# Data work of GpSimd moved to the vector and scalar engines in a two-block transformer kernel

## The chip, the cores and the metric

The kernel runs on one core of a Trainium2 chip. The metric is the device time of one execution in microseconds (us), the median of several runs. TensorE (PE) multiplies matrices, VectorE (DVE) and ScalarE (ACT) work on rows of 128 partitions, GpSimd (POOL) can do the same arithmetic, and SyncE (SP) issues most DMAs. Each engine works off its own queue of instructions in order, and engines wait for each other by semaphores.

## The reference, cut to what matters

The input is 256 tokens of 1024 numbers in single precision. A first block has two layers, each of a feed-forward part, an attention mixer, a second feed-forward part and a gate; a second block has a mixer of attention and a spatial gate, a cross attention to a memory of 256 rows, and then an expert layer that takes a third of the time:

```python
def peer_ffn(h, w_q, subkeys, w_down, w_up):          # 16384 experts, 8 heads, 16 experts per head and token
    q = (xc @ w_q).reshape(128, 8, 2, 128)
    s = jnp.einsum("thpd,hpnd->thpn", q, subkeys)
    s1, i1 = lax.top_k(s[:, :, 0], 16)
    s2, i2 = lax.top_k(s[:, :, 1], 16)
    cand_s = s1[..., :, None] + s2[..., None, :]
    cand_i = i1[..., :, None] * 128 + i2[..., None, :]
    top_s, top_pos = lax.top_k(cand_s, 16)            # over the 256 candidates of a head
    e = jnp.take_along_axis(cand_i, top_pos, axis=-1)
    g = softmax(top_s)
    a = gelu(einsum("td,thkd->thk", xc, w_down[e]))
    return einsum("thk,thkd->td", g * a, w_up[e])
```

Before every part stands a norm, `x * rsqrt(mean(x*x) + 1e-6) * g`.

## The kernel before, in words

All matrices are multiplied in three passes: a weight is split into a rounded half `wH` (ACT, a copy) and the rest `wL` (DVE, weight minus `wH`), the activations likewise into `xH` and `xL`, and PE adds `xH wH + xH wL + xL wH`. Weights come in pieces of 128 x 1024 through four buffers `raw`; `split` (L1360) makes the halves, `prefetch` two pieces ahead. The tokens are two tiles of 128, whose units of work are interleaved by `run_units` (L1381).

`rsqrt` (L475) computes a reciprocal root on one number per partition in nine small GpSimd instructions: an integer guess and three Newton steps. It follows `sumsq` (L532), a squaring on ACT that also sums. `rsqrt2` (L489) does two at once. There are 33 roots on POOL, 29 single ones and two pairs, and one on DVE; `fin1` (L1071) chains two of them for each tile, since the final norm of the first block and the first norm of the second stand one behind the other.

The expert layer does not gather. It multiplies all 16384 experts: 128 down items ("D", 24 matmuls of 256 columns each, then a gelu) and 128 up items ("U", 12 matmuls of 512 columns), with a coefficient matrix that is zero where a token did not choose an expert. For the first 96 items (`DAHEAD`, L31) there are only D items; from the 97th on, U and D alternate. During these 96 items the choice of the experts and the coefficients are computed beside the matmuls, as background units:

- `peer_sel` (L1550), for each tile of tokens: `pick` (the best 16 of 128 of the second half of the heads), `cand` (50 of the 256 candidates of a head are enough; their scores `c` and indices `e`), `top` (the best 16 of 50), `exps`, `soft`, and per head `dec` (L1596: compare the position with a counter, 16 x 50 = 800 wide, on DVE, then multiply by `e` on POOL) and `red` (a sum on DVE); `fin` and `finT` make, transposed, the indices `idx` in 16 bits and the weight split into a power of two `pow` and two half-precision parts of its mantissa.
- `peer_coef` (L1654), for each group of four tokens, 64 groups: `hot` (L1663) makes one-hot rows on DVE: a comparison of 1024 wide in 16 bits into `X` (tag `pTs`), two products of 512 into `Y` (tag `qT`), a product with `pow` of 512; `prod` (L1683) has eight small matmuls on PE, an eviction on ACT into `KT`, and after every fourth group a DMA of the coefficients to DRAM from ACT's queue.
- `prep` (L1710), for each U item: coefficient times activation (POOL, 256 wide, tag `qT`), then the split on ACT and DVE (tag `pTs`). The coefficients come back from DRAM by `load_coef` (L1705), a DMA on SP, for eight items at a time.

As long as background units are left, `split` gives 384 (`SHARE`, L38) of a piece's 1024 columns of `wL` to POOL (L1369 to L1372).

When the units are issued follows `background` (L1746): a model of three engines' free times, with costs per unit, `BG` and `SLACK`, advanced by 2.6 us for each item. Every instruction is recorded in that order; then `Plan.order` (L297) puts all of them in a final order for each engine. It simulates the engines with the costs of `times` (L202) and takes, whenever an engine is free, the instruction with the lowest number that is ready. SP's DMAs keep their order. Only the order is kept from this; on the chip, semaphores decide.

At the end, `finish`, `finish_r` and `finish_out` (L1831 to L1859) add the result, take the last norm and store it; the root of tile 0 is on POOL, that of tile 1 on DVE.

All instructions are emitted by one helper (L150), so the profile tells them apart by tile names: `wL<-raw,wH` is a split.

Of the kernel before, what the change touches and what calls it, by code (L numbers as in the profile page):

```python
# [6 lines left out]
F = mybir.dt.float32  # L7
# [24 lines left out]
BG = 1.35, 1.2, 1.4  # L32
SLACK = 3.0
# [4 lines left out]
SHARE = 384  # L38
# [163 lines left out]
def times(i):  # L202

    views = i.outs + i.reads
    n = max(columns(v) for v in views)
    small = min(size(v.dtype) for v in views) == 2
    ps = any(v.buf.space == "ps" for v in i.reads)
    if i.op == "dma_start":
        return 330, 0
    if i.eng == "tensor":  # L210
        n = columns(i.outs[0])
        if i.op == "transpose":
            return 109, 272
        if i.a[1].dtype == F:
            return (223, 388) if n > 64 else (200, 380)
        if n < 256:
            return 112, 290
        return 0.4427 * n + 5.8, 0.43 * n + 172
    if i.eng == "vector":
        if i.op in ("max", "max_index", "match_replace"):  # L220
            b = n + 60
        elif i.op in ("tensor_scalar", "tensor_copy") and not ps:
            b = 0.54 * n + 120 if n > 4 else 80
        elif small:
            b = 0.53 * n + 65
        elif n <= 32:
            b = n + 80
        else:
            b = 1.04 * n + (80 if i.op == "tensor_tensor_reduce" or not ps else 110)
        return b, b + (85 if n > 4 else 90)  # L230
    if i.eng == "scalar":
        b = 0.833 * n + (190 if "accum_out" in i.k else 100)
        return b, b + (10 if "accum_out" in i.k else 105)
    b = 2.3 * n + 250
    return b, b
# [155 lines left out]
class Body:  # L391
# [83 lines left out]
    def rsqrt(self, ss, n, out, g=None):  # L475

        g = g or self.nc.gpsimd
        w = self.sb([128, 4], F, "rsq", 3)
        g.tensor_scalar(w[:, 0:1], ss, 1.0 / n, EPS, op0=OP.mult, op1=OP.add)
        g.tensor_scalar(w[:, 2:3].bitcast(I32), w[:, 0:1].bitcast(I32), -0.5, float(0x5F3759DF),  # L480
                        op0=OP.mult, op1=OP.add)
        g.tensor_scalar(w[:, 1:2], w[:, 0:1], -0.5, None, op0=OP.mult)
        y = w[:, 2:3]
        for i in range(3):
            g.tensor_scalar(w[:, 3:4], y, y, w[:, 1:2], op0=OP.mult, op1=OP.mult)
            z = out if i == 2 else w[:, 2:3]
            g.tensor_scalar(z, w[:, 3:4], 1.5, y, op0=OP.add, op1=OP.mult)

    def rsqrt2(self, ss, ns, out):  # L489

        g = self.nc.gpsimd
        w = self.sb([128, 8], F, "rsq2", 2)
        v, xh, u = w[:, 0:2], w[:, 2:4], w[:, 4:6]
        for i in range(2):
            g.tensor_scalar(v[:, i:i + 1], ss[:, i:i + 1], 1.0 / ns[i], EPS, op0=OP.mult, op1=OP.add)
        g.tensor_scalar(out.bitcast(I32), v.bitcast(I32), -0.5, float(0x5F3759DF), op0=OP.mult, op1=OP.add)
        g.tensor_scalar(xh, v, -0.5, None, op0=OP.mult)
        for i in range(3):
            g.tensor_tensor(u, out, out, op=OP.mult)
            g.tensor_tensor(u, u, xh, op=OP.mult)  # L500
            g.tensor_scalar(u, u, 1.5, None, op0=OP.add)
            g.tensor_tensor(out, out, u, op=OP.mult)
# [29 lines left out]
    def sumsq(self, src, n, ss=None):  # L532
        ss = self.sb([128, 1], F, "ss", 4) if ss is None else ss
        self.nc.scalar.activation(self.slot("junk", 1, 512).bitcast(mybir.dt.bfloat16)[:, :n], src, AF.Square,
                                  accum_out=ss)
        return ss

    def half_rs(self, t):

        self.hr[t] = self.sb([128, 1], F, "hrs", 2)  # L540
        self.nc.gpsimd.tensor_scalar(self.hr[t], self.rs[t], 0.5, None, op0=OP.mult)

    def norm(self, t, name, src=None, rname="rs", pre=PRE, post=POST, tags="pa", fn=None, half=False):
# [12 lines left out]
        def stats(_):  # L556
            ss = self.sumsq(self.h[t] if src is None else src(t), 1024)
            self.rs[t] = self.sb([128, 1], F, f"{rname}{t}", 2)
            self.rsqrt(ss, 1024, self.rs[t])
# [1482 lines left out]
```

## Time and profile before

| | us |
|---|---|
| median of 3 runs | 2174.52 (2174.11 to 2177.05) |
| the profiled execution's own time | 2176.68 |
| its span, first to last instruction | 2174.9 |
| PE busy | 2105.7 (97%) |
| DVE busy | 1360.5 (63%) |
| ACT busy | 1158.9 (53%) |
| POOL busy | 433.1 (20%) |

The busy time of PE counts matmuls that overlap: the next begins before the last has drained. So a PE that is busy all the time can still be slower than its best pace, and the pace is read from how many matmuls a stretch holds. The mean of one DVE or ACT instruction likewise holds up to about 0.1 us in which its successor already runs.

### The profile page before, as it was taken

The numbers are of one execution on the slowest core, as the hardware profiler recorded it, in microseconds if no ns is written. First come the engines' busy times: TensorE is split into PE (matmuls) and PEld (weight loads), VectorE is DVE, ScalarE is ACT, GpSimd is POOL, SyncE is SP. The second block draws the span as 40 slices with busy tenths as digits, with TensorE's granted clock in tenths as the row PEclk, the third lists the DMA queues.
The fourth block names the chain that finished last, engine by engine and source line by source line (L and its number), as shares of the span: only waits on it lengthen the run. The fifth ranks groups of instructions, "written<-read, shape, count | busy, mean of one in ns | idle before, by whom it ended". The sixth has DMA issues, their size and how long they took to land.

```text
span 2174.9 us, 31356 instructions
## 1 busy us (share of the span) xinstructions
PE 2105.7 (97%) x11616; PEld 1775.6 (82%) x11616; DVE 1360.5 (63%) x2445; ACT 1158.9 (53%) x1787; POOL 433.1 (20%) x589
## 2 busy tenths in 40 slices
PE   8999999999999999999999999987999999999997
PEld 6888778887888887888778888887999999888886
DVE  5555655557555565555755667999979645455554
ACT  5445754446444665444655565544667544444454
POOL 1001110004000101000330112367446311122222
PEclk9999999999999999999999999999999999999999
DMA  6655336565665443666544654344767867677783
GB/s 224 210 184 167 115 116 188 183 189 174 193 184 179 148 140 101 194 184 188 192 146 141 189 164 146 107 146 156 245 208 243 265 208 226 206 230 244 230 254 125
DMA packets 138379, 398.59 MB, mean 183 GB/s; under 512 B 12912, under 2 KB 47344, under 8 KB 135920
## 3 DMA queue, kind: packets, MB, share of 16 engines
q1 hardware_dynamic: 135920, 379.80, 56.2%
q10 hardware_dynamic: 2304, 16.78, 2.2%
q8 instruction: 91, 1.49, 0.3%
q14 instruction: 64, 0.52, 0.1%
HBM read 378.71 MB, written 17.83 MB: 182 GB/s over the span
## 4 chain that ended last, share of the span: by engine, by line
PE 84%; DVE 10%; ACT 2%; issue 2%; POOL 1%; DMA 0%; SPq 0%; ACTq 0%; POOLq 0%; DVEq 0%
PE m L150 44%; PE a L150 35%; PE p L150 5%; DVE wL L150 2%; DVE pTs L150 2%; DVE qT L150 2%; DVE V L150 1%; POOL rsq L150 1%; DVE C L150 1%; DVE E L150 1%; ACT wH L150 1%; ACT xH L150 0%; ACT s L150 0%; DVE xL L150 0%; DVE junk L150 0%
## 5 line engine op out<-in xcount | busy, mean ns | idle before, releaser
L150 DVE TENSOR_TENSOR wL<-raw,wH 128x1024 fp32r<-128x1024 f32 (+2 forms) x678 | 807.1, 1193 | 634.7 <-ACT wH L150 632.4
L150 ACT ACTIVATE wH<-raw 128x1024 fp32r<-128x1024 f32 (+1 forms) x678 | 715.4, 1058 | 745.9 <-PE a L150 332.2
L150 PE MATMUL m<-wH,xH 128*128 128x512 f32 (+1 forms) x1088 | 447.4, 411 | 14.4 <-DVE s L150 5.9
L150 PE MATMUL m<-wH,xL 128*128 128x512 f32 (+1 forms) x1088 | 432.7, 398 | 0.9 <-DVE xL L150 0.9
L150 PE MATMUL m<-wL,xH 128*128 128x512 f32 (+1 forms) x1088 | 432.5, 398 | 0.9 <-DVE wL L150 0.9
L150 PE MATMUL a<-wH,pTs 128*128 128x512 f32 x1024 | 326.1, 394 | 0.0
L150 PE MATMUL m<-xH,wL 128*128 128x256 f32 x1024 | 290.4, 284 | 24.3 <-DVE wL L150 19.8
L150 PE MATMUL m<-xH,wH 128*128 128x256 f32 x1024 | 293.5, 287 | 0.0
L150 PE MATMUL m<-xL,wH 128*128 128x256 f32 x1024 | 287.8, 281 | 1.0 <-DVE xL L150 1.0
L150 PE MATMUL a<-wH,s 128*128 128x512 f32 (+1 forms) x760 | 265.8, 394 | 0.0
L150 PEld LDWEIGHTS m<-wH,xH 128*128 128x128 f32 x1088 | 206.8, 190 | 62.9 <-DVE s L150 7.4
L150 PEld LDWEIGHTS m<-wH,xL 128*128 128x128 f32 x1088 | 206.6, 190 | 49.4 <-DVE xL L150 1.5
L150 PEld LDWEIGHTS m<-wL,xH 128*128 128x128 f32 x1088 | 207.4, 191 | 42.4 <-DVE wL L150 2.0
L150 PEld LDWEIGHTS a<-wH,pTs 128*128 128x128 f32 x1024 | 192.3, 188 | 44.2
L150 POOL TENSOR_SCALAR rsq<-ss 128x1 f32<-128x1 f32 x33 | 10.9, 331 | 1089.0 <-ACT junk L150 1088.3
L150 PEld LDWEIGHTS m<-xH,wL 128*128 128x128 f32 x1024 | 193.8, 189 | 29.3 <-DVE wL L150 24.0
L150 PE MATMUL a<-wL,pTs 128*128 128x512 f32 x512 | 202.0, 394 | 0.0
L150 PEld LDWEIGHTS m<-xL,wH 128*128 128x128 f32 x1024 | 194.5, 190 | 2.9 <-DVE xL L150 1.4
L150 PEld LDWEIGHTS m<-xH,wH 128*128 128x128 f32 x1024 | 193.6, 189 | 1.4
L150 POOL TENSOR_TENSOR wL<-raw,wH 128x384 fp32r<-128x384 f32 x90 | 147.9, 1651 | 148.2 <-ACT wH L150 125.0
L150 PEld LDWEIGHTS a<-wH,s 128*128 128x128 f32 x760 | 142.5, 188 | 32.7 <-ACT E L150 0.6
L150 PE MATMUL a<-wL,s 128*128 128x512 f32 (+1 forms) x380 | 149.1, 392 | 0.0
(272 smaller groups left out, 2433.0 us busy)
## 6 DMA issues: line engine op xcount, KB each, us to landing
raw<-in_ws_dram SPq DMA_DIRECT2D x416, 512.0 KB, 3.7
raw<-in_wdn_dram SPq DMA_DIRECT2D x128, 512.0 KB, 3.7
raw<-in_wup_dram SPq DMA_DIRECT2D x128, 512.0 KB, 4.3
coef<-KT ACTq DMA_DIRECT2D x16, 1024.0 KB, 5.0
KT<-coef SPq DMA_DIRECT2D x16, 1024.0 KB, 7.9
raw<-in_ws_dram SPq DMA_DIRECT2D x4, 416.0 KB, 3.2
h<-in_x_dram SPq DMA_DIRECT2D x4, 256.0 KB, 5.1
stage<-in_alibi_dram SPq DMA_DIRECT2D x1, 1024.0 KB, 8.1
```

What stands on the lines that cost most here:

```text
L150: return getattr(getattr(nc, self.eng), self.op)(*[v.get() if isinstance(v, View) else v for v in self.a], **real)
```

## The change

Every POOL instruction that works on data in SBUF goes to another engine, except those that prepare constants (`memset`, `gfin`, the triangle of the spatial gate):

- The reciprocal root: eight DVE instructions instead of nine on POOL; the mean is already formed by ACT's squaring (`scale`), so the first step falls away, and pairs are two single roots. In `fin1` the second root is taken of a product with `other`, so that it does not wait for the first.
- The split: DVE subtracts all 1024 columns; `SHARE` is gone.
- `cand`: the nine sums of `e` go to DVE. `dec`: the comparison is made in 16 bits, its product with `e` goes to DVE.
- `hot`: the product with `pow` becomes four ACT instructions of 128 columns, each with `pow` as its scale; `pow` is kept in single precision.
- `prep`: the product goes to DVE. `xn` (a scaled copy in `peer_q`) goes to ACT. The products with the last gain in `finish`, the two small steps of the sink in `attn`, and tile 0's last root go to DVE.
- The background: instead of the model of three engines, one list (selection of tile 0; then groups of four tokens, the first 32 of them with tile 1's selection between them) of which after each item so much is issued that the DVE costs of the units are spread evenly over 90 items (`DAHEAD - SPARE`). `load_coef(0)` comes at item 93; before, three items behind the last unit.
- `times` has new costs for the order: for instance no extra price for an ACT eviction into `KT`, 97 ns for each per-partition scalar operand on ACT.

The core of the diff:

```diff
+    if i.eng == "scalar":
+        b = (0.833 * n + 50 if ps else 0.86 * n + 87) + 97 * each
...
-    def rsqrt(self, ss, n, out, g=None):
-        g = g or self.nc.gpsimd
+    def rsqrt(self, ms, out, other=None):
+        v = self.nc.vector
         w = self.sb([128, 4], F, "rsq", 3)
...
+        m, y, z = w[:, 0:1], w[:, 1:2], w[:, 2:3]
+        if other is None:
+            v.tensor_scalar(m, ms, EPS, -0.5, op0=OP.add, op1=OP.mult)
+        else:
+            v.tensor_scalar(z, other, EPS, EPS, op0=OP.add, op1=OP.mult)
+            v.tensor_scalar(m, ms, z, -0.5, op0=OP.add, op1=OP.mult)
+        v.tensor_scalar(y.bitcast(I32), m.bitcast(I32), -0.5, float(0x5F3759DF - 2 ** 30 - 2 ** 22),
                         op0=OP.mult, op1=OP.add)
         for i in range(3):
...
+            v.tensor_scalar(z, y, y, m, op0=OP.mult, op1=OP.mult)
+            v.tensor_scalar(out if i == 2 else y, z, 1.5, y, op0=OP.add, op1=OP.mult)
...
-        d = w - self.share
-        nc.vector.tensor_tensor(l[:, :d], src[:, :d], h[:, :d].bitcast(F), op=OP.subtract)
-        if self.share:
-            nc.gpsimd.tensor_tensor(l[:, d:], src[:, d:], h[:, d:].bitcast(F), op=OP.subtract)
+        nc.vector.tensor_tensor(l, src, h.bitcast(F), op=OP.subtract)
...
+                nc.vector.tensor_tensor(hit.rearrange("p k (c d) -> p k c d", d=2),
+                                        cut(self.iob[:, :NC], 2).unsqueeze(1).to_broadcast(wide),
+                                        V["tb"][:, 16 * h:16 * h + 16].unsqueeze(2).to_broadcast(wide),
                                         op=OP.is_equal)
-                nc.gpsimd.tensor_tensor(eq, eq, V["e"][:, h, :].unsqueeze(1).to_broadcast([128, 16, NC]), op=OP.mult)
+                nc.vector.tensor_tensor(eq, hit, V["e"][:, h, :].unsqueeze(1).to_broadcast([128, 16, NC]), op=OP.mult)
...
-                nc.vector.tensor_tensor(x[:, :4], x[:, :4], V["pow"][:, c].unsqueeze(2).to_broadcast(half), op=OP.mult)
+                for i in range(4):
+                    nc.scalar.activation(X[:, i, :], X[:, i, :], AF.Copy, scale=V["pow"][:, c.start + i:c.start + i + 1])
...
-        nc.gpsimd.tensor_tensor(cut(ca, 16), cut(self.act.pop(j), 16), self.cb[j // 8][:, :, j % 8, :],
+        nc.vector.tensor_tensor(cut(ca, 16), cut(self.act.pop(j), 16), self.cb[j // 8][:, :, j % 8, :],
                                 op=OP.mult)
...
+        back = s0 + [f0]
         s1.append(f1)
+        for q, u in enumerate(Hs):
+            back += [u] + s1[len(s1) * q // 32:len(s1) * (q + 1) // 32] + ([Ps[q - 1]] if q else [])
+        back.append(Ps[-1])
+        whole, spent = sum(u.cost[0] for u in back), 0.0
+        def background(part):
+            nonlocal spent
+            while back and spent <= part * whole:
+                spent += back[0].cost[0]
+                back.pop(0).fn(None)
...
+            if m < DAHEAD - 1:
+                background((m + 1) / (DAHEAD - SPARE))
+            if m == DAHEAD - SPARE + 3:
                 self.load_coef(0)
```

## Rows read from the trace of the kernel before

**Rows 1.** The page: busy time of each engine.
```profile
PE 2105.7 (97%) x11616; PEld 1775.6 (82%) x11616; DVE 1360.5 (63%) x2445; ACT 1158.9 (53%) x1787; POOL 433.1 (20%) x589
```

**Rows 2.** Windows: stretch, length, busy time (instructions) of each engine, clock, DMA.
```profile
core 0: us, PE busy (x) PEld busy (x) DVE busy (x) ACT busy (x) POOL busy (x), PEclk, DMA share, GB/s
1374.18:1716.48 342.30, 315.89 (x2833) 307.33 (x2832) 316.64 (x670) 198.80 (x233) 195.00 (x130) 0.99 0.62 203
1568.58:1581.95 13.37, 13.37 (x132) 13.20 (x130) 13.16 (x21) 9.13 (x11) 6.78 (x4) 1.00 0.70 237
1699.59:1713.65 14.06, 14.06 (x122) 14.06 (x121) 6.61 (x6) 7.37 (x10) 3.05 (x3) 1.00 0.98 329
1716.48:2164.00 447.52, 447.35 (x2306) 378.85 (x2304) 239.30 (x288) 215.87 (x305) 96.19 (x127) 1.00 0.70 218
...
1374.18:1444.60 70.42, 61.52 (x493) 58.77 (x492) 69.45 (x235) 33.11 (x45) 45.70 (x39) 1.00 0.47 150
```

**Rows 3.** Waits of PE in 1374.18 to 1716.48: total us, times, longest.
```profile
PE m L150 <- DVE wL L150: 19.8, 19, 3.0
```

**Rows 4.** DVE by form, 1374.18 to 1444.6: busy us, mean ns | idle before.
```profile
L150 DVE TENSOR_TENSOR wL<-raw,wH 128x640 fp32r<-128x640 f32 x19 | 22.6, 1187 | 0.0
L150 DVE TENSOR_TENSOR E<-c_iota,V 128x800 f32<-128x800 f32 x8 | 11.1, 1392 | 0.0
```

**Rows 5.** DVE by form, 1380 to 1720.
```profile
L150 DVE TENSOR_TENSOR qT<-pTs,rope 128x512 f16<-128x512 bf16 x128 | 73.4, 614 | 0.3
L150 DVE TENSOR_TENSOR pTs<-c_mask,rope 128x1024 bf16<-128x1024 bf16 x64 | 51.8, 810 | 1.8 <-PE p L150 1.4
```

**Rows 6.** Chain of waits, 1460 to 1530: start us, us, what.
```profile
1466.42 0.59 DVE pTs L150
1467.01 0.74 DVE wL L150
1467.75 0.67 DVE qT L150 x2
...
1496.49 0.98 DVE E L150
```

**Rows 7.** Chain of waits, 525 to 537: a whole split; timeline at 1566.
```profile
529.63 1.14 DVE wL L150
...
1566.17 0.82 DVE L150 TENSOR_TENSOR wL<-raw,wH 128x640 fp32r<-128x640 f32 x1
```

**Rows 8.** The page: POOL's first step of a root; POOL by form: its splits.
```profile
L150 POOL TENSOR_SCALAR rsq<-ss 128x1 f32<-128x1 f32 x33 | 10.9, 331 | 1089.0 <-ACT junk L150 1088.3
...
L150 POOL TENSOR_TENSOR wL<-raw,wH 128x384 fp32r<-128x384 f32 x90 | 147.9, 1651 | 148.2 <-ACT wH L150 125.0 <-DVE C L150 23.2
```

**Rows 9.** Timeline of ACT in three short stretches: start us, us, what.
```profile
229.49 0.39 ACT L150 ACTIVATE s<-s,sm 128x128 f32<-128x128 f32 x1
229.78 0.19 ACT L150 ACTIVATION_READ_ACCUMULATOR s<-s,sm 128x1 f32 x1
...
1626.47 1.99 ACT L150 ACTIVATE KT<-p 128x512 f32<-128x512 f32 x2
1629.22 1.06 ACT L150 ACTIVATE wH<-raw 128x1024 fp32r<-128x1024 f32 x1 [0.75 <-DVE pTs L150]
1630.18 0.58 ACT L150 ACTIVATE E<-m 128x512 f32<-128x512 f32 x1
1630.66 1.08 ACT L150 ACTIVATE KT<-p 128x512 f32<-128x512 f32 x1
```

**Rows 10.** Waits in 1070 to 1104, around the chained norms.
```profile
PE m L150 <- ACT C L150: 3.5, 2, 2.4
```

**Rows 11.** The tail: DVE's root in the timeline; the chain's last steps.
```profile
2166.14 1.64 DVE L150 TENSOR_SCALAR rsq<-rsq 128x1 int32<-128x1 int32 x7
...
2169.18 0.72 ACT ao L150
```

**Rows 12.** The page: DMA issues, KB each, median us to landing.
```profile
KT<-coef SPq DMA_DIRECT2D x16, 1024.0 KB, 7.9
```

More of the change, by code (lines that the diff above doesn't have):

```diff
@@ L31 @@
 DAHEAD = 96
[L32 to L33 removed]
+SPARE = 6
 SPLIT = 1.2, 1.6, 2.4
@@ L205, in times @@
     n = max(columns(v) for v in views)
-    small = min(size(v.dtype) for v in views) == 2
     ps = any(v.buf.space == "ps" for v in i.reads)
+    each = sum(isinstance(x, View) and columns(x) == 1 for x in (*i.a[2:], i.k.get("scale"), i.k.get("bias"),
+                                                                 i.k.get("in_to_replace")))
     if i.op == "dma_start":
@@ L214, in times @@
         if i.a[1].dtype == F:
-            return (223, 388) if n > 64 else (200, 380)
+            return (223, 388) if n > 64 else (196, 380)
         if n < 256:
[L217 to L230, printed above, removed]
-    if i.eng == "scalar":
[L232 to L235, printed above, removed]
+            return (112, 290) if i.a[1].dtype == R else (56, 297)
+        return 0.442 * n + 5, 0.43 * n + 172
+    if i.eng == "scalar":
+        b = (0.833 * n + 50 if ps else 0.86 * n + 87) + 97 * each
+        return (b + 100, b + 200) if "accum_out" in i.k else (b, b + 108)
+    if i.eng == "gpsimd":
+        b = 2.35 * n + 140 + 75 * each
+        return b + 50, b + 50
+    if i.op in ("max", "max_index", "match_replace"):
+        b = n + {"max": 62, "max_index": 72, "match_replace": 131}[i.op]
+    elif n <= 32:
+        b = n + 75 + 60 * each + (120 if i.op == "reciprocal" else 0)
+    elif i.op == "tensor_scalar" and not ps:
+        b = 0.54 * n + 124
+    elif i.op == "tensor_copy":
+        b = 1.05 * n + 120 if ps else 0.71 * n + 43
+    elif all(size(v.dtype) == 2 for v in views):
+        b = 0.53 * n + 65
+    else:
+        b = 1.05 * n + 67 + 60 * each
+    return b, b + 83
 def table(i, now):
@@ L712, in fn @@
                 if sink is not None:
-                    nc.gpsimd.tensor_tensor(sm[:, 3], sink(g), mx, op=OP.subtract)
+                    nc.vector.tensor_tensor(sm[:, 3], sink(g), mx, op=OP.subtract)
                 st[g] = (s, sm)
@@ L848, in e0 @@
             ss = self.sb([128, 2], F, "ss2", 2)
-            self.sumsq(V["e0"][:, :256], 256, ss[:, 0:1])
-            self.sumsq(V["e0"][:, 256:384], 128, ss[:, 1:2])
+            self.meansq(V["e0"][:, :256], 256, ss[:, 0:1])
+            self.meansq(V["e0"][:, 256:384], 128, ss[:, 1:2])
             r = self.sb([128, 2], F, "rqkv", 2)
-            self.rsqrt2(ss, (256, 128), r)
+            for i in range(2):
+                self.rsqrt(ss[:, i:i + 1], r[:, i:i + 1])
             V["rq"], V["rkv"] = r[:, 0:1], r[:, 1:2]
@@ L1735, in experts @@
         room, nring = [], 0
+        self.iob = self.mask.bitcast(B16)[:, :128]
+        nc.vector.tensor_copy(self.iob, self.iota)
         (s0, f0), (s1, f1) = self.peer_sel(0), self.peer_sel(1)
[L1737 to L1738 removed]
+        Hs, Ps = self.peer_coef()
+        back = s0 + [f0]
         s1.append(f1)
[L1740 to L1763 removed]
+        for q, u in enumerate(Hs):
[7 more added lines that the diff above has]
+                back.pop(0).fn(None)
         for m, (kind, j) in enumerate(self.items):
[L1765 removed]
             if m == DAHEAD - 1:
[L1767 to L1770 removed]
+                background(1.0)
                 for i in range(2):
@@ L1824, in experts @@
                 nc.scalar.activation(cut(pair, 256), ps, AF.Gelu_apprx_tanh)
-            if any(bg):
-                background(2.6 * (m + 1))
-                filled = m
-            elif 0 not in self.cb and m >= filled + 3:
+            if m < DAHEAD - 1:
+                background((m + 1) / (DAHEAD - SPARE))
+            if m == DAHEAD - SPARE + 3:
                 self.load_coef(0)
```

130 lines of the change are left out of this document (37 added, 93 removed).

## The prediction

> **What bounds the kernel now.** I read the busy times first, then windows, then what PE waits for. PE is busy for 97% of the span [rows 1], so time can only come back where PE is late, and the windows show where. From 1716 us on, in 447.5 us with U and D items, PE is busy for all but 0.2 us [rows 2]; nothing that another engine saves there is worth anything. The stretch that matters is the 342.3 us of the first 96 items, from the first D matmul to the first U matmul. Its floor is read from the pace: with little beside it, five items (120 matmuls of the 122 in the row) took 14.06 us, 2.81 each; four items with eight small product matmuls each took 13.37 us, 3.34 each, so a group of products costs 0.53 [rows 2]. Floor: 96 x 2.81 + 64 x 0.53 = 269.8 + 33.9 = 303.7 us. The stretch took 38.6 us more. The wait of PE with the largest total there is for `wL` from DVE, 19.8 us [rows 3] (the rest is slowed pace, which counts as busy), and DVE is busy for 316.6 of the 342.3 us [rows 2]. So PE is bound by DVE in the selection and by itself elsewhere.
>
> **Why DVE is late.** The same operations have two prices. In the selection the split of 640 columns took 1.19 us on average [rows 4], where the chain has it at 0.74; a product of 512 in 16 bits 0.61 [rows 5] against 0.335 (two in 0.67); the comparison of 1024 0.81 against 0.59 [rows 5, 6]. The difference is not DVE's own work: POOL's 384 columns of the same split take 1.65 us and run beside it 90 times [rows 8]. A mean holds some overlap with the next instruction, 0.08 (0.82 in the timeline, 0.74 in the chain for the same split [rows 6, 7]); less that, 19 x 0.37 in the first 70 us and 128 x 0.20 + 64 x 0.14 in the groups make 7 + 26 + 9 = 42 us of DVE time lost to POOL, without the later splits.
> The Trainium skill says why (SBUF — State Buffer, "Who interferes with whom"): a VectorE instruction with two SBUF inputs and a GpSimd instruction that reads SBUF exclude each other for a whole instruction. This trace agrees with its 1.19 against 0.74. By that rule all of it goes with the POOL work.
> If the two engines merely shared a rate, the moved columns would cost DVE as much as they free, and the stretch would stay near 342 us, which is the rival of no change below.
>
> **The change part by part, the 96 items.** The units' own costs set the pacing: tile 0's selection is 31.05, a group 1.3, tile 1's selection 31.05, together 145.3 over 90 items, 1.614 per item. So tile 0's selection lies on items 0 to 19 (stage A), 32 groups with tile 1's selection on the next 45 (B), the other 32 groups on the next 26 (C); then 6 items without background.
>
> Stage A, before: 70.4 us with DVE busy 69.45 [rows 2]; 20 items at 2.81 are 56.2, so 14.2 us of the loss lie here. DVE after: 69.45, less 19 x (1.19 - 0.82) = 7.0 and 8 x (1.39 - 0.98) = 3.3 of collisions [rows 4, 6], less 8 x (0.98 - 0.46) = 4.2 for the comparison in 16 bits (0.59 x 800/1024 [rows 6]), less 7 of tile 1's picks and candidates that now come later and 3 of collisions of small operations (estimates: a fifth and a twelfth of the 35.7 that are neither splits nor comparisons); plus 20 x (1.14 - 0.74) = 8.0 for whole splits [rows 6, 7], 8 x 0.98 = 7.8 for the products with `e` (bounds 0.46, as a 16-bit operation, and 1.39, the collided row; I take 0.98, the same 800 in single precision), 1 for nine small sums. Sum 61.8, over 56.2 by 5.6; I take a loss of 7, between 0 (DVE's backlog moves into B) and 16 (nothing freed but the comparison).
> Stage B: DVE 45 x 1.14 + 32 x (0.59 + 0.67) + a selection of 61.8 - 20 x 1.14 = 39 gives 51.3 + 40.3 + 39 = 131; PE 45 x 2.81 + 32 x 0.53 = 143.4. PE covers it by 12 us; I allow 2 for a late split, bounds 0 and 6.
> Stage C turns to ACT. A weight copy holds ACT 0.96 us (1629.22 to 1630.18), a gelu 0.48 for two items (1630.18 to 1630.66), an eviction into `KT` 0.86 to 1.1 (two in 1.99, the second 1.13) [rows 9]. A power is an operation that the trace does not have; the nearest is the exponential of 128 columns with a per-partition operand, 0.29 from its start to the next instruction's [rows 9]. Its low bound is an eighth of the weight copy, 0.12, the high one the exponential's whole 0.39. At 0.29: 26 x (0.96 + 0.24) + 32 x (4 x 0.29 + 0.86) = 31.2 + 64.6 = 95.8 against PE's 26 x 2.81 + 32 x 0.53 = 90.0, a loss of 6. At 0.12 none; at 0.39 with 1.08 evictions 31.2 + 84.5 = 115.7, a loss of 26. The order is made with 0.833 x 512 + 50 = 477 ns for these evictions, so it will not see this. DVE has 26 x 1.14 + 40.3 = 70 here, no bound.
> The Trainium skill speaks against this edit (ScalarE: Activation LUTs, "Rules for kernel authors"): a multiplication belongs on VectorE, up to three times as fast in 16 bits. Row for row it is 4 x 0.29 = 1.16 us on ACT for one product of 512 at 0.335 on DVE; by that rule the edit would cost most, which is the ACT rival.
> The hand-over: the coefficients take 7.9 us to come back from DRAM [rows 12], and `load_coef(0)` is now issued two items later than before, and the product that waits for it stands in DVE's queue, in front of splits that PE needs two items on, no longer in POOL's. I take 1 us, bounds 0 and 4.
> Loss after: 7 + 2 + 6 + 1 = 16 against 38.6: 22.6 us faster. With the low ends 38.6; with the high ends 16 + 6 + 26 + 4 = 52, 13 slower.
>
> **Elsewhere.** The chained roots of `fin1`: PE waits 3.5 us for an eviction [rows 10] that waits for `rs` from POOL. On DVE seven of a root's steps took 1.64 us, 0.235 each [rows 11]; eight are 1.9, and the second no longer follows the first. I take 3, bounds 0 (DVE's other work between the steps) and 3.5.
> The tail: the last ACT scaling begins at 2169.18 behind POOL's root of tile 0 [rows 11], while DVE's root of tile 1 is done one step behind its seven, at 2168.0 [rows 11]. With tile 0's root on DVE, during the last matmuls, the end waits for the latter, which also loses a step: 1.5 us, bounds 0 and 2.
> The other roots put 33 x 1.9 = 63 us on DVE, and `prep` 128 x about 0.33 (a quarter of the whole split's 1.14 is 0.29 [rows 7], and some fixed part; estimate) = 42 us behind 1716 us. There DVE is busy for 239 of 447 us [rows 2], so PE hides it; without that cover it would be 0.33 per item pair, 42. The `xn` copies on ACT (4 x 0.58, as a 512-wide eviction [rows 9]) and the sink's small steps are hidden likewise; at nothing.
> Sum: 22.6 + 3 + 1.5 = 27 us off the profiled execution's 2176.7 us, 2149.6. That execution is 2.2 above the median of 2174.5, so in terms of runs: 2147.5, and I say 2148.
>
> **Rivals.**
> All hidden (26%): A's backlog flows into B and a power costs near 0.12; losses 4 in all, 35 + 4.5 = 39 us: 2135. For it: B has 12 us to spare. Against: the order sees A saturated, and ACT's operand costs.
> ACT becomes the bound (14%): C loses 26 instead of 6, as above, by long evictions: 2148 + 20 = 2168. For it: 1.08 and 1.13 in the rows. Against: the 1.99 for two. The Trainium skill's rule on multiplications, above, stands on this rival's side.
> No change (6%): DVE's slow rows are its own; then moving work onto it gains only what the comparison and the powers give, and the roots take that back: 2174. Against: 0.74 and 1.19 are the same instruction.
> Slower (8%): the roots block the splits. Eight dependent steps in DVE's queue hold a split back for up to 1.9 us, and PE has two pieces in hand; at 33 places [rows 8] this decides once a root costs PE more than 27/33 = 0.8 us; at the whole 1.9 it is 63 - 27 = 36 us slower, 2210; at 1.1 2184. Against: at the norms the order can put a split between two steps, and PE's cover of two items is 5.6 us.
> The forecast has 46%, its own range 2141 to 2157.
>
> **Numbers.** 0.2%, 4.3 us, is about what a measurement of this kernel can tell from no change. Faster: 46 + 26 + 14 = 86%; same 6%; slower 8%. The range goes from 2132, just under the all-hidden case, to 2170, just over the ACT case.
>
> **What would show it.** POOL nearly empty; the split of 1024 at 1.22 us (1.14 + 0.08) everywhere in the first 96 items, products at 0.42 instead of 0.61; the stretch from the first D to the first U matmul at about 320 us, with PE's waits for `wL` in its first 60 us and waits behind ACT in its last 90; PE's wait around the chained norms under 1 us. A stretch above 340 us, powers above 0.35 us, or new waits of PE for `wL` at the norms would make the prediction wrong.

## The result, and the profile after

The changed kernel takes 2154.22 us (median of four runs, 2153.36 to 2155.99), beside 2175.62 of the kernel before (2174.11 to 2177.05): ratio 0.9903, interval 0.9886 to 0.9920. The forecast was 2148, its own range 2141 to 2157. The profiled execution took 2155.99 us with a span of 2154.2, 20.7 less than the span before.

The page's busy line first, then windows of the first 96 items cut at items 20, 65 and 91, and what stands behind them up to the last matmul (from and to, length, busy time of PE, PEld, DVE, ACT and POOL, granted clock, DMA):

```profile
PE 2108.7 (98%) x11616; PEld 1780.3 (83%) x11616; DVE 1415.9 (66%) x2828; ACT 1228.0 (57%) x2047; POOL 6.2 (0%) x16
```

```profile
1382.02:1442.05 60.03, 59.06 (x492) 58.37 (x491) 58.39 (x184) 32.55 (x43) 0.00 (x0) 1.00 0.53 176
1442.05:1586.90 144.85, 144.85 (x1336) 143.51 (x1334) 132.68 (x324) 126.06 (x236) 0.00 (x0) 1.00 0.66 221
1586.90:1684.30 97.40, 92.17 (x892) 89.98 (x889) 74.56 (x125) 95.89 (x200) 0.00 (x0) 1.00 0.65 225
1684.30:1698.64 14.34, 14.34 (x124) 14.34 (x122) 6.13 (x5) 7.46 (x9) 0.00 (x0) 1.00 0.80 255
...
1698.64:2146.24 447.60, 447.24 (x2306) 379.35 (x2304) 294.87 (x426) 217.41 (x309) 0.00 (x0) 1.00 0.68 221
```

POOL is empty in all of them. From the first D matmul to the end of the 96th item it took 342.3 us [rows 2] and takes 316.6; here and below this is "the stretch". In the kernel before, the first U matmul stands at its end. In the changed kernel, the matmuls of a 97th D item come in between, and the first U matmul starts 2.8 us later (a row of PE's timeline):

```profile
1701.46 0.40 PE L148 MATMUL a<-wH,pTs 128*128 128x512 f32 x1
```

DVE, which was busy for 93% of the stretch, is busy for 86%; now ACT is full, for 95.89 of 97.40 us in items 65 to 90. PE's waits in 1382 to 1700 (total, times, longest) say the same:

```profile
PE p L148 <- ACT KT L148: 5.2, 7, 1.4
PE m L148 <- DVE wL L148: 0.4, 1, 0.4
```

The 19.8 us for DVE's `wL` [rows 3] are 0.4, and 5.2 us for ACT's `KT` evictions are new. Gone, too, is a wait of the kernel before that [rows 3] doesn't show, for POOL's own columns of the splits (`PE m L150 <- POOL wL L150: 4.5, 4, 1.4`). The operations of DVE in 1382 to 1698 (busy us, mean ns | idle before), which answer to [rows 4, 5]:

```profile
L148 DVE TENSOR_TENSOR wL<-raw,wH 128x1024 fp32r<-128x1024 f32 x96 | 117.0, 1218 | 38.9 <-ACT wH L148 38.5
L148 DVE TENSOR_TENSOR qT<-pTs,rope 128x512 f16<-128x512 bf16 x128 | 48.8, 416 | 0.6
L148 DVE TENSOR_TENSOR pTs<-c_mask,rope 128x1024 bf16<-128x1024 bf16 x64 | 43.2, 682 | 2.1 <-PE p L148 2.0
L148 DVE TENSOR_TENSOR E<-junk,C 128x800 f32<-128x800 bf16 x16 | 15.7, 982 | 0.0
...
L148 DVE TENSOR_TENSOR junk<-c_mask,V 128x800 bf16<-128x800 bf16 x16 | 9.1, 566 | 0.0
```

A split of all 1024 columns takes 1.22 us, as the one of 640 beside POOL did in the first 70 us (1.19 [rows 4]); the product fell from 0.61 to 0.42 us and the comparison from 0.81 to 0.68.

Not everything came back. On the spans, in order of time: the first D matmul starts 7.8 us **later** (1382.02 against 1374.18), the stretch is 25.7 shorter, from there to the last matmul 0.3 longer (447.62 against 447.35), what follows the last matmul 3.1 shorter (7.94 against 11.07): 7.8 - 25.7 + 0.3 - 3.1 = -20.7.

### The profile page after: what moved, and what is told of

Read it like the earlier page. It is cut to its first block, busy times and chain, and to the rows that moved or that the text cites. A ratio compares the mean times of both kernels' runs of the same rounds, so it can differ in the third digit from the quotient of the medians.

```text
span 2154.2 us, 31186 instructions
## 1 busy us (share of the span) xinstructions
PE 2108.7 (98%) x11616; PEld 1780.3 (83%) x11616; DVE 1415.9 (66%) x2828; ACT 1228.0 (57%) x2047; POOL 6.2 (0%) x16
## 3 DMA queue, kind: packets, MB, share of 16 engines
q8 instruction: 91, 1.49, 0.3%
## 4 chain that ended last, share of the span: by engine, by line
PE 88%; ACT 6%; DVE 3%; issue 1%; DMA 1%; ACTq 0%; SPq 0%
PE m L148 49%; PE a L148 34%; PE p L148 5%; ACT wH L148 2%; ACT pTs L148 1%; ACT KT L148 1%; DVE xL L148 1%; DVE wL L148 1%; ACT xH L148 1%; DVE rsq L148 1%; ACT s L148 1%; DVE s L148 0%; DMA coef<-KT 0%; DVE h L148 0%; ACT C L148 0%
## 5 line engine op out<-in xcount | busy, mean ns | idle before, releaser
L148 DVE TENSOR_TENSOR wL<-raw,wH 128x1024 fp32r<-128x1024 f32 (+1 forms) x678 | 826.7, 1220 | 573.7 <-ACT wH L148 572.5
L148 PE MATMUL m<-wH,xH 128*128 128x512 f32 (+1 forms) x1088 | 448.0, 412 | 11.5 <-DVE s L148 4.6
L148 PEld LDWEIGHTS a<-wL,pTs 128*128 128x128 f32 x512 | 96.2, 188 | 20.8
L148 ACT ACTIVATE s<-m,rs 128x256 f32<-128x256 f32 x88 | 41.7, 474 | 89.3 <-PE m L148 88.6
```

The source lines that it names most:

```text
L148: return getattr(getattr(nc, self.eng), self.op)(*[v.get() if isinstance(v, View) else v for v in self.a], **real)
```

## The experiments

In the table "loss" is what a stretch takes over the floor of the prediction, 2.81 us for an item and 0.53 for each product group that begins in it, cut at the first matmuls of the items. "First D" is the start of the first D matmul. First D, stretch and losses are those of one profiled execution, the median is of four. The kernel before, run again beside the others, took 2176.14 (e1 to e4), 2177.17 (e5 to e8) and 2176.22 us (e9 to e12), so about 1 us between rows of different groups need not come from the kernels.

| kernel | median us (range) | ratio to before, interval | first D | stretch | loss 0-19 | 20-64 | 65-90 |
|---|---|---|---|---|---|---|---|
| before | 2175.62 (2174.11-2177.05) | 1 | 1374.2 | 342.3 | 14.4 | 21.7 | 2.4 |
| changed | 2154.22 (2153.36-2155.99) | 0.9903, 0.9886-0.9920 | 1382.0 | 316.6 | 3.7 | 2.0 | 6.9 |
| e1 roots on POOL | 2141.78 (2140.34-2145.61) | 0.9845, 0.9829-0.9862 | 1370.4 | 315.7 | 3.5 | 1.4 | 6.9 |
| e2 xn on POOL | 2152.14 (2148.75-2155.21) | 0.9886, 0.9869-0.9902 | 1380.9 | 316.7 | 3.7 | 2.0 | 6.9 |
| e3 splits shared | 2164.13 (2161.80-2166.39) | 0.9945, 0.9929-0.9962 | 1381.1 | 324.7 | 8.0 | 6.5 | 6.1 |
| e4 powers on DVE | 2148.49 (2146.20-2149.87) | 0.9876, 0.9860-0.9893 | 1379.3 | 309.9 | 3.7 | 2.0 | 0.1 |
| e5 = e1 + e2 + e4 | 2131.16 (2130.47-2131.86) | 0.9790, 0.9774-0.9807 | 1365.8 | 308.5 | 3.5 | 1.4 | -0.2 |
| e6 four roots on POOL | 2150.33 (2147.40-2152.57) | 0.9882, 0.9866-0.9899 | 1372.5 | 317.0 | 3.7 | 2.0 | 7.2 |
| e7 = e1 + dummy steps | 2143.57 (2142.20-2145.07) | 0.9850, 0.9834-0.9866 | 1367.9 | 316.0 | 3.5 | 1.7 | 6.9 |
| e8 before, whole splits | 2164.43 (2163.53-2165.09) | 0.9945, 0.9928-0.9961 | 1371.5 | 331.8 | 13.2 | 15.5 | -0.7 |
| e9 = e5 + old decoding | 2145.82 (2145.29-2146.10) | 0.9861, 0.9845-0.9878 | 1368.7 | 320.4 | 11.4 | 5.4 | -0.2 |
| e10 = e5 + fp32 comparison | 2135.61 (2134.76-2137.67) | 0.9815, 0.9799-0.9831 | 1367.3 | 312.6 | 6.3 | 2.4 | -0.1 |
| e11 = e5 + old pacing | 2138.14 (2137.13-2139.56) | 0.9827, 0.9810-0.9843 | 1367.5 | 314.2 | 6.9 | 3.5 | 0.0 |
| e12 = e5, chained roots on DVE | 2130.41 (2128.68-2131.55) | 0.9788, 0.9771-0.9804 | 1365.7 | 308.5 | 3.5 | 1.4 | -0.2 |

The first four undo one part of the change each.

**e1, all roots but the last two on GpSimd again**, the same eight steps:
```
     def rsqrt(self, ms, out, other=None, end=False):
-        v = self.nc.vector
+        v = self.nc.vector if end else self.nc.gpsimd
```


> The kernel after, with all reciprocal roots but the two at the very end on GpSimd again (same eight steps). Theory A (the eight steps stand in DVE's queue in front of work that PE waits for; that costs the 6 us between 200 and 270 us, in the even mixer, and wins 4 us at the chained norms): the even mixer gets 4 to 6 us faster, the chained norms 3 to 5 slower, the rest stays; 2150 to 2156 us. Rival (the 6 us come from the new order of the even mixer alone, its costs or the sink's steps, not from the roots): the even mixer stays as slow, the chained norms lose 3 to 5; 2157 to 2160 us.

12.4 us faster than the changed kernel, more than either theory had: the roots on DVE, which the prediction had hidden at no cost, are the largest loss. The start of the D items moves by 11.7 us and the rest hardly. Measured from one matmul to another, the same two in both kernels, e1 is faster by 7.1 us in the even mixer (the attention of the first block's first layer, 200 to 280 us in the changed kernel), by 3.9 in the odd mixer (that of its second layer, 700 to 780) and by 2.1 from 1290 to the first D, and slower by 2.1 at the chained norms (1060 to 1120). Theory A had 4 to 6 in the even mixer and 3 to 5 at the chained norms; neither theory had the other two places. The widest wait that the roots cause lies in the even mixer (PE's waits from 205 to 280 us):

```profile
PE p L148 <- DVE rsq L148: 2.9, 1, 2.9
```

That view names the last thing released. DVE's timeline there shows what it is (start us, us, engine, operation, out<-in, idle before):

```profile
250.30 0.26 DVE L148 TENSOR_SCALAR rsq<-rsq 128x1 f32<-128x1 f32 x1
250.49 0.15 DVE L148 TENSOR_TENSOR sm<-c_ev_sinks,sm 128x4 f32<-128x4 f32 x1
251.23 0.42 DVE L148 CUSTOM_DVE_ANT_0 s<-a,stage 128x256 f32<-128x256 f32 x1 [0.60 <-PE a L148]
...
251.58 0.21 DVE L148 TENSOR_SCALAR rsq<-rsq 128x1 f32<-128x1 f32 x1
...
252.30 0.27 DVE L148 TENSOR_SCALAR rsq<-rsq 128x1 int32<-128x1 int32 x2
...
252.55 0.27 DVE L148 TENSOR_SCALAR rsq<-rsq 128x1 f32<-128x1 f32 x1
...
253.50 0.42 DVE L148 TENSOR_TENSOR xL<-p,xH 128x256 fp32r<-128x256 f32 x1
253.84 0.20 DVE L148 TENSOR_SCALAR rsq<-rsq 128x1 f32<-128x1 f32 x1
```

A step of a root at 250.30, then one of the sink, then the masked scores that wait 0.60 us for PE; only behind them does the root go on, and the `xL` on which PE's next products wait stands behind the whole queue. PE has nothing from 251.2 to 254.1.

**e2, `xn` on GpSimd again:**
```
-                nc.scalar.activation(V["xn"][hf], self.h[t][:, 512 * hf:512 * hf + 512], AF.Copy, scale=self.rs[t])
+                nc.gpsimd.tensor_scalar(V["xn"][hf], self.h[t][:, 512 * hf:512 * hf + 512], self.rs[t], None,
+                                        op0=OP.mult)
```


> The kernel after, with the scaled copy xn of the expert queries on GpSimd again. Theory A (on ACT the two copies stand in front of the eviction that frees PE's bank, 3 us at 1324): the stretch from 1304 to 1330 gets 3 us faster, total 2150 to 2152 us. Rival (the 3 us are DVE's root or the order): the wait of PE at 1324 stays above 1 us and the total at 2154.

2.1 us in the median, with overlapping ranges, just past Theory A's 2150 to 2152. In the trace the stretch 1304 to 1329 us loses 0.3 us to the kernel before instead of 3.1, so the place is right. The changed kernel's chain of waits has it (start, us, what):

```profile
1323.67 0.37 ACT xH L148
1324.03 1.22 ACT s L148 x2
1325.25 0.59 ACT qT L148
1325.88 2.42 PE m L148 x6
```

The two copies into `s` are `xn`; PE waits for the `qT` eviction behind them.

**e3, GpSimd subtracts 384 columns of each split again** while there is background:
```
-        nc.vector.tensor_tensor(l, src, h.bitcast(F), op=OP.subtract)
+        d = w - (384 if self.share and w == PIECE else 0)
+        nc.vector.tensor_tensor(l[:, :d], src[:, :d], h[:, :d].bitcast(F), op=OP.subtract)
+        if d < w:
+            nc.gpsimd.tensor_tensor(l[:, d:], src[:, d:], h[:, d:].bitcast(F), op=OP.subtract)
```


> The kernel after, with GpSimd again subtracting 384 of 1024 columns of each weight split while background units are left. Theory A (the collisions of GpSimd with DVE made the selection slow): although DVE has 0.4 us less to do for each split, the 96 items take 330 to 342 us instead of 317, total 2167 to 2180 us. Rival (the even portions won the time, the engine of the columns does not matter): DVE is relieved, the 96 items stay at 313 to 318 us, total 2150 to 2155.

9.9 us slower, 8.1 of it in the stretch: the direction of Theory A but short of its ranges (330 to 342 and 2167 to 2180), and far from the rival's. DVE's forms, 1382 to 1698 us:

```profile
L148 DVE TENSOR_TENSOR wL<-raw,wH 128x640 fp32r<-128x640 f32 x91 | 84.0, 924 | 25.8 <-ACT wH L148 25.7
L148 DVE TENSOR_TENSOR pTs<-c_mask,rope 128x1024 bf16<-128x1024 bf16 x64 | 61.6, 970 | 3.2 <-PE p L148 3.1
L148 DVE TENSOR_TENSOR qT<-pTs,rope 128x512 f16<-128x512 bf16 x128 | 59.2, 506 | 0.6
```

Giving 384 columns away saves DVE 91 x 0.294 = 26.8 us on the splits and costs it 64 x 0.288 = 18.4 on the comparisons and 128 x 0.090 = 11.5 on the products: 3 us more work in all, for a third of the columns less. A mean hides what happens. Each of these operations comes in two sizes (duration in ns, min/median/max):

```profile
L148 DVE TENSOR_TENSOR pTs<-c_mask,rope x64: 666/687/1523, 1445.2 to 1682.4; 128x1024 bf16<-128x1024 bf16 x64
L148 DVE TENSOR_TENSOR qT<-pTs,rope x128: 400/416/1255, 1447.7 to 1684.3; 128x512 f16<-128x512 bf16 x128
```

In the changed kernel no comparison takes more than 0.69 and no product more than 0.43 us. Here 40 of 64 comparisons are like that, 22 take 1.49 to 1.52, and 2 are in between; of the products 114 are like that and 14 take 1.23 to 1.26. So one that has to wait takes 0.82 us longer, whatever its own length. One of the 22 in the timeline:

```profile
1603.43 0.82 DVE L148 TENSOR_TENSOR wL<-raw,wH 128x640 fp32r<-128x640 f32 x1
1603.47 1.65 POOL L148 TENSOR_TENSOR wL<-raw,wH 128x384 fp32r<-128x384 f32 x1 [6.51 <-DVE qT L148]
...
1604.17 1.50 DVE L148 TENSOR_TENSOR pTs<-c_mask,rope 128x1024 bf16<-128x1024 bf16 x1
```

POOL's subtraction begins while DVE's runs and takes 1.65 us, where the shortest took 1.01; DVE's next operation stands beside it until it ends at 1605.12 and needs 0.55 us more. All 36 long ones began beside a subtraction of POOL that ended 0.94 to 0.97 us after their start.

**e4, the power's product on the vector engine again:**
```
-                for i in range(4):
-                    nc.scalar.activation(X[:, i, :], X[:, i, :], AF.Copy, scale=V["pow"][:, c.start + i:c.start + i + 1])
+                nc.vector.tensor_tensor(x[:, :4], x[:, :4], V["pow"][:, c].unsqueeze(2).to_broadcast(half), op=OP.mult)
```


> The kernel after, with the product with the powers on DVE again (one product of 512 in 16 bits instead of four ACT instructions for each group of four tokens). Theory A (ACT binds the last third of the 96 items, loss 6.9 us): that loss falls under 2, DVE takes 64 x 0.335 = 21 us more, of which the middle third may lose 0 to 4; total 2146 to 2152 us. Rival (PE waits there for the eviction into KT and its two banks whatever the powers cost): the loss stays above 5, total 2153 to 2156.

5.7 us faster, as Theory A has it; the loss in items 65 to 90 goes from 6.9 to 0.1. ACT in the changed kernel, 1586.9 to 1684.3 us, and a piece of its timeline:

```profile
L148 ACT ACTIVATE pTs<-pTs,V 128x128 bf16<-128x128 bf16 x128 | 42.3, 391 | 1.0 <-ACT pTs L148 1.0
L148 ACT ACTIVATE KT<-p 128x512 f32<-128x512 f32 x32 | 33.8, 1064 | 0.3 <-ACT pTs L148 0.3
```

```profile
1619.87 1.26 ACT L148 ACTIVATE pTs<-pTs,V 128x128 bf16<-128x128 bf16 x4
1621.04 0.57 ACT L148 ACTIVATE E<-m 128x512 f32<-128x512 f32 x1
1621.51 1.05 ACT L148 ACTIVATE KT<-p 128x512 f32<-128x512 f32 x1
1622.38 0.36 ACT L148 ACTIVATE pTs<-pTs,V 128x128 bf16<-128x128 bf16 x1
```

Four powers hold ACT from 1619.87 to 1621.04, 0.29 each; the eviction behind them from 1621.51 to 1622.38, 0.87.

The next four ask whether these add up, what a root costs by, and what the splits alone give.

**e5, the three parts undone together** (the edits of e1, e2 and e4).

> The changed kernel with three of its parts undone together: the norm roots on GpSimd, xn on GpSimd, the power product on the vector engine; the whole splits, the e products, the 16-bit comparison, the even pacing and the last two roots stay as changed. Alone these took 12.4, 2.1 and 5.7 us off 2154.2. Theory A (three separate places: the mixers, the query norm, items 65 to 90): the gains add, 2133 to 2137, with the stretch from the first D to the first U matmul at 308 to 311 us and its start at 1368 to 1371. Rival (two of them pay for the same wait, or an earlier start is given back in the selection): 2139 to 2143.

2131.16: 23.1 us faster than the changed kernel, where the three parts alone gave 12.4 + 2.1 + 5.7 = 20.2. They add, with 2.9 us to spare: the time is 1.8 below Theory A's range. This is the fastest but for e12.

**e6, only the two roots of each tile's even mixer on GpSimd** (`self.rsqrt(ss[:, i:i + 1], r[:, i:i + 1], pool=True)` in `e0`).

> The changed kernel with only the two roots that each tile of the even mixer takes (of its compressed query and key) on GpSimd; all other roots stay on the vector engine. Theory A (a root costs only where its result, or what stands behind it in the vector engine's queue, is needed at once): the even mixer gives back about 6 us of the 12.4 that all roots give: 2146 to 2150, and its stretch (200 to 270 us) is as before or better. Rival B (every root costs some 0.4 us wherever it stands): four of 33 roots give 1.5 us, 2152 to 2154.

2150.33, just over Theory A's range and 3.9 us under the changed kernel: four roots of 32 give a third of the 12.4 us, where Theory B had 1.5 (its 2152 to 2154 overlaps the range of the four runs). In the profiled execution, the fastest of the four, the even mixer (matmuls from 200 to 280 us) gives back 5.4 us, while the odd mixer (710 to 756), whose roots are still on DVE, takes 2.9 more than in the changed kernel. The lower clock takes 5.1 us there instead of 3.4; e2, with the same instructions in that place as the changed kernel, also has 5.1, so executions differ in this. The place of a root matters more than the number.

**e7, e1 with eight independent vector steps beside each root:**
```
+        if not end:
+            u = self.sb([128, 8], F, "dummy", 2)
+            for i in range(8):
+                self.nc.vector.tensor_scalar(u[:, i:i + 1], ms, 1.5, -0.5, op0=OP.add, op1=OP.mult)
```


> The kernel with the norm roots on GpSimd, and beside each root eight vector instructions of the same size that read the same mean square and write eight separate columns that nobody reads: the vector engine issues as many small steps as in the changed kernel, but none waits for the one before it. Theory A (what costs is that each step waits for the last while the queue stands behind it): at most 8 x 0.08 = 0.6 us per root and mostly hidden, 2141 to 2146, near the 2141.8 without them. Rival B (the number of instructions on the vector engine costs, by its time or by where the planner puts other work): 2149 to 2154, as in the changed kernel.

1.8 us over e1, within the runs' ranges and Theory A's, and 10.7 under the changed kernel. The added steps are there, all 256 (duration min/median/max):

```profile
L148 DVE TENSOR_SCALAR dummy<-ss x256: 134/143/233, 11.8 to 1312.7; 128x1 f32<-128x1 f32 x128
```

So the number of small steps on DVE is not the price. Their time is tested less well: DVE is busy for 1373.2 us in e1, 1389.4 here and 1415.9 in the changed kernel, so these steps add 16.2 us where the roots add 42.7. If that time were the price, 16.2/42.7 of the 12.4 us, 4.7, would be expected here; 1.8 came. What differs besides is that a root's steps each wait for the one before, in a queue where other work stands between and behind them, and that results hang on them. Whether the held-up queue or the late result weighs more, this run doesn't part; the timeline under e1 shows both.

**e8, the kernel before with whole splits** (`SHARE = 0`), one part of the change alone.

> The kernel before with one part of the change alone: the vector engine subtracts all 1024 columns of each split during the background too (share 0), all else as before. Theory A (most of the loss was the collision of the two engines on the splits and the products beside them): the stretch from the first D to the first U matmul falls from 342 to 322 to 332 us, time 2156 to 2167. Rival B (the other parts, the 16-bit comparison and the even pacing, gave most): the stretch stays at 336 to 346, time 2170 to 2180.

12.7 us faster than the runs of before on the same chip (2177.17), the stretch 10.5 shorter: in Theory A's range, for the stretch at its long end (331.8). The whole split gives less than half of the 25.7 (the expectation of e9 has 10.7 for these 10.5).

The last four go from e5 and look for the rest of it.

**e9 and e10, the decoding back:** in e10 only the comparison in single precision, in e9 also its product with `e`, and the candidates' sums, on GpSimd (in the diff, e9's):
```
-                nc.vector.tensor_tensor(eq, hit, V["e"][:, h, :].unsqueeze(1).to_broadcast([128, 16, NC]), op=OP.mult)
+                nc.vector.tensor_tensor(eq, self.iota[:, :NC].unsqueeze(1).to_broadcast([128, 16, NC]),
+                                        cut(V["tf"], 16)[:, h, :].unsqueeze(2).to_broadcast([128, 16, NC]),
+                                        op=OP.is_equal)
+                nc.gpsimd.tensor_tensor(eq, eq, V["e"][:, h, :].unsqueeze(1).to_broadcast([128, 16, NC]), op=OP.mult)
```


> The kernel with the three parts undone (2131.2; 308.5 us from the first D to the first U matmul, loss 4.9), with the old decoding besides: comparison in single precision, the product with e and the candidates' e sums on GpSimd. What the splits (10.7 of the 25.7 us by the run with whole splits alone) and the powers leave open is some 22 us of loss that this, or the pacing, has to hold. Theory A (each GpSimd product over 800 columns holds up the vector operations beside it, as the 384 columns of the splits did): stretch 314 to 322, time 2137 to 2145. Rival B (the vector engine has 16 products less to do, and the stretch has cover): 306 to 310, 2129 to 2133.

> The same kernel with only the comparison back in single precision, its product with e on the vector engine. Theory A: 16 comparisons of 800 columns cost the vector engine about 0.5 us more each, 4 us per tile, of which tile 0's fall on its nearly full 60 us: stretch 309 to 312, time 2131 to 2135. Rival B (the 16-bit form was most of what is left open): stretch above 314, time above 2137.

e10: stretch 4.1 us longer, time 4.5 over e5, both just past the long end of Theory A and short of Theory B. e9: another 7.8 us of stretch (312.6 to 320.4), Theory A, with the time 0.8 past its range. Sixteen products of 800 columns and the small sums on GpSimd cost PE these 7.8 us, though DVE no longer does them; 1.7 of them are a clock of 0.66 in 1432 to 1437 us. DVE's longest comparison of 1024 takes 2.25 us here and its longest product 2.00, more than beside POOL's 384 columns in e3.

**e11, the old handing out of the background** (the functions of the kernel before, no operation changed):
```
-            if m < DAHEAD - 1:
-                background((m + 1) / (DAHEAD - SPARE))
+            if any(bg):
+                background(2.6 * (m + 1))
```


> The kernel with the three parts undone, with the old handing out of the background units (costs, slack and due times instead of even portions; coefficients loaded three items after the last one); no operation differs. Theory A (the old pacing puts tile 0's selection and the groups with tile 1's selection too thick for the vector engine and leaves the end thin): stretch 314 to 324, time 2137 to 2147. Rival B (pacing is worth nothing once the operations are cheap): 307 to 311, 2130 to 2134.

Stretch 5.7 us longer, time 7.0 over e5: Theory A, at its low edge. The first 20 items take 63.1 us with DVE busy for 61.12, in e5 59.7 with 58.26:

```profile
1367.45:1430.55 63.10, 60.59 (x495) 58.74 (x494) 61.12 (x194) 33.06 (x45) 0.00 (x0) 1.00 0.53 170
```

**e12, e5 with the chained roots of `fin1` on the vector engine.**

> The kernel with the three parts undone, but the chained roots of fin1, which the next matmuls wait for with nothing else to do, on the vector engine. Theory A (a root belongs where its own latency is the wait on an idle vector queue, and only there): 2 us less than 2131.2, 2127 to 2130, the stretch 1079 to 1114 us 2 us shorter. Rival B (their steps hold up other vector work there as elsewhere): 2131 to 2134.

The stretch 1079 to 1114 us is 2.1 us shorter than in e5, as Theory A has it; the time is 0.75 less with overlapping ranges, so in the total it can't be told from none.

## Why the prediction was right, and where it was not

The time came within the forecast's own range by its main term, and 6 us over the predicted value because of one term set to nothing. That it is no further off is partly luck: without the chained norms, the first D item comes 12 us later than before, where the prediction had nothing, and three terms gave 5.9 us more than forecast (25.7 for 22.6 in the 96 items, 4.2 for 3 at the chained norms, 3.1 for 1.5 in the tail).

**The 96 items: as forecast, with the same three causes.** The prediction had losses of 7, 2 and 6 in stages A, B and C, and 1 for the hand-over; the trace has 3.7, 2.0 and 6.9, and 0.3. For the hand-over, PE's wait of 0.36 us for `pTs` behind the first U matmul comes on top; the 97th D item in front of it gave the coefficients 2.8 us that the prediction did not count with. Its unit costs held: the split 1.22, the product 0.42, the product with `e` 0.98 (in A the value chosen between 0.46 and 1.39). In C the prediction worked out 95.8 us of ACT against 90.0 of PE; ACT was busy for 95.89 and PE's floor left a loss of 6.9, and e4 shows that it was ACT: undone, the loss is 0.1. A was put 3.3 too high, since DVE was busy for 58.39 us where the sum had 61.8; which of its estimates was too high no run separates.

**What the gain is made of.** From e5's loss of 4.9 up, putting back one part at a time: GpSimd's columns of the splits 8.1 (e3) or, from the other side, 10.5 (e8); the products with `e` and the candidates' sums on GpSimd 7.8 (e9 against e10); the single-precision comparison 4.1 (e10); the old pacing 5.7 (e11). That is 25.7 to 28.1, and 4.9 with them is 30.6 to 33.0 of the 38.6 before; the 5.6 to 8.0 left over no run assigns to a part. Some of all this is PE's clock behind its waits: in the kernel before the windows 1452 to 1458 and 1486 to 1492 us, with granted clocks down to 0.50, lack 3.4 us, and 1414 to 1420 in e3 lacks 1.7; e5 and the changed kernel have 1.00 in the whole stretch. The prediction put DVE's slow rows down to POOL's columns of the splits; POOL's products with `e` it did not price as a cause, and the comparison and the pacing it had in stage A alone (4.2 and 7 us of DVE). The splits are the largest part, but they are a third of it, with three others beside them.

**The collision.** e3 shows it: with POOL at 384 columns a comparison takes either 0.68 us or 1.50, and a product 0.42 or 1.24. The Trainium skill (SBUF — State Buffer, "Who interferes with whom") has the two engines shut each other out for whole instructions; the trace of e3 agrees with its two sizes 0.82 us apart. Engines that merely share a rate would slow every overlapped operation somewhat; here 13 of the 40 short comparisons overlap a subtraction of POOL, too, and are no longer than the rest. The rival that moved columns merely trade places is wrong by the 8.1 us.

**The step that failed: "The other roots put 33 x 1.9 = 63 us on DVE ... PE hides it ... at nothing", and `xn` with them.** By e1 the roots cost 12.4 us net, the chained ones counted, which gain; by e2 `xn` costs about 2. The number of the steps was not the point (e7: as many steps without the dependence cost 1.8). In the even mixer PE has no matmul left that waits for nothing: there a step of a root in DVE's queue comes behind masked scores that wait for PE, and PE's next `xL` behind the root, and PE stands for 2.9 us. For the odd mixer the traces show no such wait (PE's waits from 700 to 745 us are 1.3 us against 0.9 in e1), so how the roots cost time there stays open, but for the clock below. The prediction's slower rival is near this, a queue held up by dependent steps, but it held up splits: PE's waits for `wL` at the norms did not come, the one for `rsq` did. Its threshold was 0.8 us per root; 12.4 over the 32 roots moved is 0.39, half of it. It was weighed at 33 norms with a cover of two weight pieces and given 8%; places without such cover, such as the even mixer, were not looked at.

**More than half of the price is the clock.** After PE's idle stretch in the even mixer its granted clock goes to the lower of its two levels, 1.2 GHz (windows of the changed kernel: length, busy times, then the clock):

```profile
251.00:254.00 3.00, 0.20 (x2) 0.00 (x1) 2.77 (x20) 2.78 (x13) 0.00 (x0) 1.00 0.05 16
254.00:256.00 2.00, 1.25 (x7) 1.03 (x8) 2.00 (x9) 1.28 (x4) 0.00 (x0) 0.68 0.00 0
256.00:258.00 2.00, 2.00 (x11) 1.96 (x11) 1.50 (x12) 0.39 (x3) 0.00 (x0) 0.50 0.70 250
258.00:260.00 2.00, 2.00 (x11) 2.00 (x10) 0.31 (x4) 1.19 (x2) 0.13 (x1) 0.50 0.03 12
260.00:262.00 2.00, 2.00 (x11) 1.77 (x10) 1.37 (x6) 0.00 (x0) 0.00 (x0) 0.61 0.00 0
```

PE is busy throughout from 256 to 260, at half speed. The same place in e5:

```profile
248.00:251.00 3.00, 1.65 (x13) 1.27 (x12) 2.23 (x15) 2.97 (x11) 2.02 (x8) 1.00 0.61 175
251.00:254.00 3.00, 2.78 (x24) 2.34 (x23) 2.66 (x14) 2.41 (x9) 0.16 (x1) 1.00 0.00 0
254.00:256.00 2.00, 2.00 (x12) 1.69 (x11) 1.34 (x10) 1.57 (x6) 0.00 (x0) 1.00 0.00 0
```

In windows of 2 us, adding each window's length times what the clock lacks to 1: from 210 to 280 us the changed kernel loses 3.4 us so, the kernel before 1.7, e5 none; over the four places with waits (210-280, 700-800, 1060-1120, 1300-1380) 11.9, 6.8 and 1.7, and e1 5.1. Of the 11.7 us by which the D items start earlier in e1 than in the changed kernel, 6.8 are clock, and only 1.7 are idle time: up to there PE is idle for 31.0 us (1351.04 of 1382.02 busy) and in e1 for 29.3 (1341.06 of 1370.37). The other 3.2 are slower pace. Single falls of the clock differ between executions of the same instructions: in the even mixer, e1 and e5 have the same roots on POOL and PE busy for 1.58 and 1.65 us of 248 to 251, and then e1's clock is 0.58 in 251 to 254 and e5's 1.00. But the sum is no accident of one execution: over the whole kernel the four runs of the changed kernel have granted clocks of 0.992 to 0.993, those of e1 0.994 to 0.997 and those of e5 0.995 to 0.996.

**The chained norms** gained 4.2 us in the trace (3 forecast, bounds 0 and 3.5), 1.7 of it clock (3.4 us lacking in 1060 to 1120 before, 1.7 now); by e1 and e12 the engine is worth 2.1 of it. In 1070 to 1104 the wait for `C` fell from 3.5 [rows 10] to 1.9, not under 1 as the prediction had it:

```profile
PE m L148 <- ACT C L148: 1.9, 1, 1.9
```

**The tail** gained 3.1 against 1.5, and the 1.5 was right: from the last matmul to the last scaling it is 3.9 us now (2146.24 to 2150.11, the row below) and was 5.3 (2163.84 to 2169.18 [rows 11]).

```profile
2148.19 1.33 ACT L148 ACTIVATE ao<-ao,rf 128x512 f32<-128x512 f32 x2 [0.38 <-DVE rf L148]
...
2150.11 0.72 ACT L148 ACTIVATE ao<-ao,rf 128x512 f32<-128x512 f32 x1 [0.59 <-DVE rf L148]
```

The rest lies in the output's transfers. Busy DMA tenths in 40 equal slices, of the kernel before from 2168 to 2175 us and of the changed one from 2148 to 2155:

```profile
DMA  0000001000000001999999999999999600000000
```

```profile
DMA  0000000000899999981299999997000000000000
```

Before, all four transfers left together and filled some 16 slices of 0.175 us. Now tile 0's pair goes first and tile 1's second, so behind the last scaling only one pair is to be moved.

**Hidden as said:** `prep` on DVE behind the 96 items. DVE is busy there for 294.87 us instead of 239.30 [rows 2], and PE for all but 0.36 of 447.60. Of the signs that the prediction named, one more than the chained norms did not come: the 3.7 us lost in the first 20 items are 0.97 of idle PE, only 0.4 of it for `wL`, and slower pace.

## What to carry to other kernels

Work on an idle engine is not free when that engine shares memory with the bound one, so look at what the neighbours of each instruction cost, not only at who is busy. But a chain of small dependent steps belongs on an engine that nothing else queues on: in this kernel the slower empty queue was better by 12.4 us than the faster full one, and only at the chained norms worse. And "hidden behind the busy engine" has to be asked place by place: a 98% busy PE still had short places where another engine's delay showed, at one of them more than twice over, 2.9 us of waiting and 3.4 of clock.

## What the runs showed of the hardware

- DVE's two-input operations and POOL's subtraction do not slow each other, they wait for each other: in e3 a comparison of 1024 takes 0.68 or 1.50 us, a product of 512 0.42 or 1.24, a split of 640 mostly 0.82 or 1.64.
- An idle stretch of PE can cost more than its own length: behind the 2.9 us in the even mixer the windows from 254 to 262 lack 0.64 + 1.00 + 1.00 + 0.78 = 3.4 us of clock. Not every wait is followed by that: e5 has one of 2.2 us between 1358 and 1362 us, with the clock at 1.00 there and in the windows behind it up to 1374. What decides, these runs don't settle.
- A power, 128 columns in 16 bits with a per-partition scale, holds ACT 0.29 us, so four cost 1.17 where DVE did the 512 columns in 0.42 (e4: 64 in 27.2 us). The Trainium skill (ScalarE: Activation LUTs, "Rules for kernel authors") puts multiplications on VectorE; the 5.7 us of e4 agree.
- One step of a root took 0.24 us on DVE and 0.34 on POOL (medians), and POOL's roots were still the better ones.
